# Hybrid encoder block on one core: the value projection and its convolution move behind the attention output's projections, a gate's projection moves beside the attention

## The chip, the cores and the metric

The kernel runs on one core of one Trainium2 chip. The metric is the device time of one execution in microseconds; the time of a kernel is the median of its runs.

## The reference, cut to what matters

One layer over 512 tokens with 1024 features, everything in float32. The normalised input h is multiplied by one wide matrix, whose columns are cut into the parts that the branches use:

```
h  = rmsnorm(x)
aq, ak, av = silu(causal_conv4(h @ W[q, k, v]))     # branch A, 512 columns each
oA = gated_delta_rule(l2norm(aq), l2norm(ak), av, g, beta)   # chunks of 64 tokens
oA = rmsnorm(oA) * silu(h @ W[z])
oB = top-128 attention(h @ W[b_q, b_k, b_v, i_q, i_k, i_w])  # branch B
x  = x + (sigmoid(h @ W[gate_a]) * (oA @ P_A) + sigmoid(h @ W[gate_b]) * (oB @ P_B)) @ W_out
x  = x + mixture_of_experts(rmsnorm(x))             # 16 experts, 2 per token
out = rmsnorm(x)
```

The convolution runs along the tokens over four taps, for each of the 1536 q, k and v features on its own. The delta rule solves one unit-triangular system per head and chunk of 64 tokens.

## The kernel before

**Projections.** A product with 512 columns of W is a "chunk" of four steps. A step takes 256 rows of W (512 KB from memory into a tile `raw`), splits them into a high and a low part (`split`: `whi` on ScalarE, `wlo` on VectorE or, as the string LOWS says, on GpSimd), and issues 24 matmuls, three for each product, into four PSUM banks (`acc`, four buffers). The split of the next step is issued a step ahead. After the last step each bank is evacuated: gate chunks by a Tanh on ScalarE; q, k and v chunks by `conv`; z by a copy, a Tanh and a VectorE product.

**conv.** For each of the four banks ScalarE copies the bank to `xrb` (L448) and a scaled copy to `xh` (L450); VectorE adds three shifted products (L452, 512 columns); after the fourth bank four Silu (L457) write the result. `xh` lies in the four buffers with tag `cv`, as do z's tiles `zt`.

**Order of the chunks.** kv, iq, then beside index scores, selection of keys and attention: bq, qk0, v, qk1, gb0 and gb1. In `behind_projections` each of these 24 steps advances the selection (PICKS), the attention (LOOKS) and the norms (NORMS) by the listed number of pieces. Selection is a chain of VectorE instructions (L595, L596). Then come pb0 and pb1 (attention output by P_B, with `systems`, which builds the triangular systems and sends their diagonal blocks to memory, `lane_n`); ga0 and z; ga1; and the delta rule (`solve`, `chain`).

**sides, lanes, clear_TT, lanes_back.** `sides(g)` has four pieces for each of two groups of heads: four transposes of k and v on TensorE (L920, L921), three VectorE products (L924 to L926), two GpSimd products (L928) and four memsets. `lanes` loads the diagonal blocks (`LN`), inverts them in 31 pairs of VectorE instructions (L952, L953), each of which needs the one before, and writes the result to memory (`lane_x`). `clear_TT` zeroes tiles TT0 and TT1 in the buffers of q and k (kq0, kq1), and TT2 and TT3 in one of h's; `lanes_back` brings the inverses there from `lane_x`, eight DMAs for two tiles. `solve` begins with TT0.

**Who decides the order in a queue.** All instructions are traced first; the framework then writes out each engine's queue: of what its model holds ready, it takes what was traced first. On the chip each engine runs its queue in order.

In the kernel before, `sides` advances by one piece of each group in each step of ga0, and `lanes` by 0, 2, 4, 4 pairs in ga0's steps and 5, 5, 5, 6 in z's.

Of the kernel before, what the change touches and what calls it, by code (L numbers as in the profile page):

```python
# [7 lines left out]
F32 = mybir.dt.float32  # L8
F32R = mybir.dt.float32r
I32 = mybir.dt.int32  # L10
AF = mybir.ActivationFunctionType
OP = mybir.AluOpType
# [6 lines left out]
T = 4  # L19
# [9 lines left out]
SELS = (13, 14)  # L29

LOWS = "DDDDDDDDDDDDPPDPPPPPPPPPPPPPPPPP"
PICKS = (1, 5, 5, 4, 4, 4, 4, 2, 2, 4, 4, 4, 2, 3, 4, 4, 3, 0, 0, 0, 0, 0, 0, 0)
LOOKS = (0, 0, 0, 0, 0, 0, 0, 0, 1, 1, 1, 4, 2, 3, 4, 4, 4, 5, 5, 4, 5, 5, 4, 4)
NORMS = (0, 0, 0, 0, 0, 0, 0, 0, 0, 1, 1, 1, 1, 1, 1, 0, 0, 2, 1, 1, 1, 1, 2, 2)

A_Q, A_K, A_V, A_Z, A_B = 0, 512, 1024, 1536, 2048
B_Q, B_K, B_V, I_Q, I_K, GATE_A, GATE_B = 2064, 2576, 2704, 2832, 3344, 3416, 4440
# [61 lines left out]
def body(tc, x, positions, norm1_g, w_in, w_proj_a, w_proj_b, w_out, norm2_g,  # L99
         w_exp_gate, w_exp_up, w_exp_down, final_norm_g, small, const, out, dbg=None):  # L100
    nc = tc.nc
    dbg = dbg or {}
    PE, ACT, DVE, POOL, SP = nc.tensor, nc.scalar, nc.vector, nc.gpsimd, nc.sync
# [115 lines left out]
    plan, raws, ready, state = [], [], [], {"at": 0, "limit": None}  # L219
    win = w_in[0]  # L220

    def want(key, src, nk, cols, *lo):

        for sub in range(nk // 2):
            plan.append((key, [src[sub * 256:(sub + 1) * 256, c:c + m] for c, m in cols], lo[sub % len(lo)]))

    low = lambda s: [POOL if c == "P" else DVE for c in s]
# [1 line left out]
    want("iq", win, 8, [(I_Q, 512)], *low(LOWS[4:8]))  # L229
    want("bq", win, 8, [(1992, 456)], *low(LOWS[8:12]))  # L230
    want("qk0", win, 8, [(A_Q, 256), (A_K, 256)], *low(LOWS[12:16]))
    want("v", win, 8, [(A_V, 512)], *low(LOWS[16:20]))
    want("qk1", win, 8, [(A_Q + 256, 256), (A_K + 256, 256)], *low(LOWS[20:24]))
    for hf in range(2):
        want(f"gb{hf}", win, 8, [(GATE_B + 512 * hf, 512)], *low(LOWS[24 + 4 * hf:28 + 4 * hf]))
    for hf in range(2):
        want(f"pb{hf}", w_proj_b[0], 4, [(512 * hf, 512)], DVE)
    want("ga0", win, 8, [(GATE_A, 512)], DVE)
    want("z", win, 8, [(A_Z, 456)], DVE)
    want("ga1", win, 8, [(GATE_A + 512, 512)], DVE)  # L240
    for hf in range(2):
# [137 lines left out]
    def tick(bg):  # L379
        for gen, n in bg:  # L380
            for _ in range(n):
                next(gen, None)

    def drain(*gens):
        for g in gens:
            for _ in g:
                pass
# [31 lines left out]
    def feat_chunk(*a, bg=()):  # L419
        for _ in feat_gen(*a):  # L420
            tick(bg)

    HT = lambda k: (hTh[k // 4][:, k % 4, :], hTl[k // 4][:, k % 4, :])
# [3 lines left out]
    cw = SM("conv").rearrange("p (b k) -> p b k", k=4)  # L427
# [10 lines left out]
    vT = [vT2[p // 2][:, p % 2, :] for p in range(4)]  # L438
    kq = [Ft([128, T, 2, 128], F32, f"kq{p}", f"kq{p}") for p in range(4)]

    xrb = Ft([128, 4, 512], F32, "xrb", "tg0")

    waiting = []

    def conv(blk, fb, acc, dst):

        xr = xrb[:, fb]
        ACT.activation(xr, acc, AF.Copy)  # L448
        xh = Ft([128, 512], F32, "xh", "cv", 4)
        out = ins_of(ACT.activation(xh, acc, AF.Copy, scale=cw[:, blk, 3:4]))  # L450
        for j in (1, 2, 3):
            DVE.scalar_tensor_tensor(xh[:, j:], xr[:, :512 - j], cw[:, blk, 3 - j:4 - j], xh[:, j:], op0=OP.mult, op1=OP.add)  # L452
        waiting.append((dst, xh.rearrange("p (t c) -> p t c", t=T) if len(dst.shape) == 3 else xh))
        if fb == 3:
            with after_(out):
                for d, v in waiting:
                    ACT.activation(d, v, AF.Silu)  # L457
            waiting.clear()

    def qk_chunk(g, bg):  # L460
        def ev(fb, acc):
            p = 2 * g + fb % 2
            conv(p if fb < 2 else 4 + p, fb, acc, kq[p][:, :, 1 if fb < 2 else 0, :])
        feat_chunk(f"qk{g}", 8, HT, ev, bg=bg)


# [270 lines left out]
                turn(2 + u // 2)  # L737
            yield from att_value(*res[u])

    gb = [Ft([128, 4, 512], F32, f"gb{hf}", f"tg{hf}") for hf in range(2)]  # L740

    def gate_gen(hf):
        def ev(fb, acc):
            j = 8 + hf * 4 + fb
            ACT.activation(gb[hf][:, fb, :], acc, AF.Tanh, bias=bgh[:, j:j + 1], scale=0.5)
        return feat_gen(f"gb{hf}", 8, HT, ev)
# [5 lines left out]
    def gate_spill(hf):  # L752
        def ev(fb, acc):
            if hf == 0:
                tg = Ft([128, 512], F32, "tga", "cv", 4)
            else:
                if fb % 2 == 0:
                    spare.append(Ft([128, 2, 512], F32, "tga", f"kq{2 + fb // 2}"))
                tg = spare[-1][:, fb % 2]
            ACT.activation(tg, acc, AF.Tanh, bias=bgh[:, hf * 4 + fb:hf * 4 + fb + 1], scale=0.5)  # L760
            SP.dma_start(gad[hf, :, fb, :], tg)
        return feat_gen(f"ga{hf}", 8, HT, ev)
# [4 lines left out]
    def behind_projections():  # L767

        for i, n in enumerate(PICKS):
            tick([(sel, n), (att, LOOKS[i]), (nrm[i // 16], NORMS[i])])  # L770
            yield

    bg = [(behind_projections(), 1)]
    tok_chunk("bq", 8, range(T), HT, ev_w3, bg=bg)
    qk_chunk(0, bg)
    feat_chunk("v", 8, HT, lambda fb, acc: conv(8 + fb, fb, acc, vT[fb]), bg=bg)
    qk_chunk(1, bg)
    drain(nrm[0])
    for _ in gate_gen(0):
        tick(bg)  # L780
    drain(sel)

# [46 lines left out]
    DVE.tensor_tensor(flat(dl), ps[:, 32:64], flat(nG), op=OP.add)  # L829
    ACT.activation(dl, dl, AF.Exp)  # L830

    for _ in gate_gen(1):
        tick(bg)
    drain(att, nrm[1])
    for g in range(2):
# [121 lines left out]
    TT = {}  # L957

    def clear_TT(t):
        if t < 2:  # L960
            TT[t] = Ft([128, 8, 128], F32, f"TT{t}", f"kq{t}")
            POOL.memset(TT[t], 0.0)
        else:
            tt = Ft([128, 2, 8, 128], F32, "TT2", "H10")
            POOL.memset(tt, 0.0)
            TT[2], TT[3] = tt[:, 0], tt[:, 1]

    def lanes_back(tiles):
# [130 lines left out]
    def z_chunk():  # L1099
        def ev(t, acc):  # L1100
            z = Ft([128, 512], F32, f"zt{t}", "cv", 4)
            zt[t] = z
            zg = GP([128, 512], name="zg", tag="E", bufs=2)
            ACT.activation(z[:, 0:456], acc[:, :456], AF.Copy)
            POOL.tensor_copy(z[:, 456:512], ztail[:, t, :])
            ACT.activation(zg, z, AF.Tanh, scale=0.5)
            DVE.scalar_tensor_tensor(z, zg, 1.0, z, op0=OP.add, op1=OP.mult)
        return tok_gen("z", 8, range(T), HT, ev)
# [9 lines left out]
    rk0 = G([128, T, 1024], name="rk0")  # L1118
# [8 lines left out]
    rk1 = [Ft([128, 2, 1024], F32, f"rk1{i}", ("obh", "obl")[i]) for i in range(2)]  # L1127
    place(1, [ke_[1][:, t] for t in range(T)], [rk1[t // 2][:, t % 2] for t in range(T)])
    side, lane = [sides(g) for g in range(2)], lanes()
    for n, _ in zip((0, 2, 4, 4), gate_spill(0)):  # L1130
        tick([(side[0], 1), (side[1], 1), (lane, n)])
    drain(*side)
    for t in range(2):
        clear_TT(t)
    for n, _ in zip((5, 5, 5, 6), z_chunk()):
        tick([(lane, n)])
    drain(lane)

    angz = GP([128, 64], name="angz")
# [2 lines left out]
    for t in range(T):  # L1142
        zv = zt[t].rearrange("p (h d) -> p h d", h=8)
        POOL.tensor_tensor(zv, zv, angz[:, None, :].to_broadcast([128, 8, 64]), op=OP.mult)
    lanes_back((0, 1))
    drain(gate_spill(1))
    feed(state["at"] + 2)
    clear_TT(2)
    lanes_back((2, 3))
# [101 lines left out]
    for fb in range(4):  # L1251
        acc = acc_tile()
# [24 lines left out]
    nm, ex, sums, wn = e1([T, 2], "nm"), e1([T, 24], "exl"), e1([T, 3], "sums"), e1([T, 16], "wn")  # L1277
# [84 lines left out]
    for sub in range(4):  # L1362
        feed(NIN + sub + 2)
        hi, lo, n = ready[NIN + sub]
# [336 lines left out]
    for e in range(16):  # L1701
        acc = acc_tile()
# [110 lines left out]
```

## Time and profile before

| | |
|---|---|
| median of 3 runs | 702.06 us (698.96 to 703.22) |
| the profiled execution | 701.66 us, span of the core 699.8 us |
| TensorE busy in the span | 655.5 us |
| VectorE busy | 526.5 us |
| ScalarE busy | 411.6 us |
| GpSimd busy | 205.0 us |
| granted TensorE clock, mean | 0.980 |

The span is the time from the first to the last instruction of the profiled execution; the other 1.86 us lie around it. The granted clock is the share of TensorE's full speed. Matmuls of 512 columns are recorded with some 0.39 us each but start every 0.23 us, so a busy TensorE need not be a TensorE at its best.

### The profile page before, as it was taken

The numbers are of one execution on the slowest core, as the hardware profiler recorded it, in microseconds if no ns is written. First come the engines' busy times: TensorE is split into PE (matmuls) and PEld (weight loads), VectorE is DVE, ScalarE is ACT, GpSimd is POOL, SyncE is SP. The second block draws the span as 40 slices with busy tenths as digits, with TensorE's granted clock in tenths as the row PEclk, the third lists the DMA queues.
The fourth block names the chain that finished last, engine by engine and source line by source line (L and its number), as shares of the span: only waits on it lengthen the run. The fifth ranks groups of instructions, "written<-read, shape, count | busy, mean of one in ns | idle before, by whom it ended". The sixth has DMA issues, their size and how long they took to land.

```text
span 699.8 us, 10563 instructions
## 1 busy us (share of the span) xinstructions
PE 655.5 (94%) x3460; PEld 538.0 (77%) x3460; DVE 526.5 (75%) x1166; ACT 411.6 (59%) x734; POOL 205.0 (29%) x259
## 2 busy tenths in 40 slices
PE   3999999799899999999999999989999999999992
PEld 2888777567676777778889988878887888888871
DVE  4567799999956466569934666774689999999875
ACT  5345456398968965433333432344258998999863
POOL 2000327516322303231071111660151432333102
PEclk9999999999899999999999999999999999999996
DMA  8333311113021112234355002979779999998963
GB/s 271 118 96 102 91 60 61 60 32 92 29 90 31 61 60 69 76 92 133 92 149 192 2 2 94 380 231 303 256 252 338 333 297 302 300 279 269 282 230 123
DMA packets 84026, 110.77 MB, mean 158 GB/s; under 512 B 17435, under 2 KB 57883, under 8 KB 83840
## 3 DMA queue, kind: packets, MB, share of 16 engines
q1 hardware_dynamic: 79360, 101.70, 44.4%
q0 software_dynamic: 4320, 7.77, 4.5%
q8 instruction: 28, 0.46, 0.3%
q10 hardware_dynamic: 288, 0.59, 0.3%
q14 instruction: 30, 0.25, 0.1%
HBM read 101.22 MB, written 16.78 MB: 169 GB/s over the span
## 4 chain that ended last, share of the span: by engine, by line
PE 70%; DVE 16%; ACT 4%; issue 4%; POOL 3%; DMA 2%; POOLq 0%; ACTq 0%; DVEq 0%
PE acc L129 53%; PE pm L129 7%; DVE xh L452 3%; PE pm L1546 2%; DVE sn L596 2%; DVE ltmp L952 2%; PE po L129 2%; DVE m L595 1%; DVE wlo L154 1%; DVE X L953 1%; POOL wlo L154 1%; POOL mTl L1227 1%; DMA xe<-h2d,ids 1%; PE pg L129 1%; PE ssq L129 1%
## 5 line engine op out<-in xcount | busy, mean ns | idle before, releaser
L153 ACT ACTIVATE whi<-raw 128x1024 fp32r<-128x1024 f32 (+1 forms) x123 | 126.7, 1048 | 99.1 <-PE acc L129 81.2
L154 DVE TENSOR_TENSOR wlo<-raw,whi 128x1024 fp32r<-128x1024 f32 (+1 forms) x100 | 124.1, 1264 | 45.1 <-ACT whi L153 35.3
L154 POOL TENSOR_TENSOR wlo<-raw,whi 128x1024 fp32r<-128x1024 f32 x23 | 57.2, 2489 | 124.6 <-ACT whi L153 116.6
L129 PE MATMUL acc<-whi,xhl 128*128 128x512 f32 x256 | 91.3, 410 | 0.3 <-DVE xhl L1553 0.3
L129 PE MATMUL acc<-hTh,wlo 128*128 128x512 f32 x224 | 89.3, 400 | 1.7 <-POOL wlo L154 1.1
L129 PE MATMUL acc<-hTh,whi 128*128 128x512 f32 x224 | 89.9, 402 | 0.8 <-ACT zb L649 0.8
L129 PE MATMUL acc<-hTl,whi 128*128 128x512 f32 x224 | 89.0, 397 | 0.0
L129 PEld LDWEIGHTS acc<-whi,xhl 128*128 128x128 f32 x256 | 48.1, 188 | 10.2 <-DVE xhl L1553 0.8
L129 PEld LDWEIGHTS acc<-hTh,wlo 128*128 128x128 f32 x224 | 42.6, 190 | 11.6 <-POOL wlo L154 1.7
L129 PEld LDWEIGHTS acc<-hTh,whi 128*128 128x128 f32 x224 | 42.8, 191 | 10.1 <-ACT zb L649 1.0
L129 PE MATMUL acc<-wlo,xhl 128*128 128x512 f32 x128 | 50.4, 394 | 0.0
L129 PEld LDWEIGHTS acc<-hTl,whi 128*128 128x128 f32 x224 | 42.8, 191 | 9.0 <-issue 0.9
L129 PE MATMUL acc<-whi,hTh 128*128 128x456 f32 (+1 forms) x120 | 45.5, 386 | 0.0
L129 PE MATMUL acc<-whi,hTl 128*128 128x456 f32 (+1 forms) x120 | 45.1, 376 | 0.0
L129 PE MATMUL acc<-wlo,hTh 128*128 128x456 f32 (+1 forms) x120 | 44.8, 374 | 0.1
L1591 POOL DMA_INDIRECT accd<-yb,ids x14 | 23.9, 1705 | 58.7 <-ACT ah L153 58.7
L1390 POOL DMA_INDIRECT xe<-h2d,ids x15 | 22.5, 1498 | 42.6 <-PE pm L1546 35.9
L452 DVE SCALAR_TENSOR_TENSOR xh<-xrb,sm,xh 128x511 f32<-128x511 f32 (+2 forms) x36 | 29.8, 879 | 0.0
L129 PE MATMUL acc<-whi,mTh 128*128 128x512 f32 (+1 forms) x72 | 27.9, 388 | 1.8 <-DVE ma L1221 1.8
L595 DVE MAX8 m<-sn 128x8 f32<-128x256 f32 (+2 forms) x48 | 26.6, 557 | 1.1 <-POOL sn L588 0.3
L129 PE MATMUL acc<-whi,mTl 128*128 128x512 f32 (+1 forms) x72 | 27.2, 378 | 0.0
L129 PEld LDWEIGHTS acc<-wlo,xhl 128*128 128x128 f32 x128 | 24.2, 189 | 3.7
(469 smaller groups left out, 1615.6 us busy)
## 6 DMA issues: line engine op xcount, KB each, us to landing
raw<-in_w_in_dram SPq DMA_DIRECT2D x24, 512.0 KB
raw<-in_w_exp_gate_dram SPq DMA_DIRECT2D x42, 256.0 KB
raw<-in_w_exp_up_dram SPq DMA_DIRECT2D x42, 256.0 KB
raw<-in_w_exp_down_dram SPq DMA_DIRECT2D x21, 512.0 KB
raw<-in_w_in_dram SPq DMA_DIRECT2D x16, 256.0 KB
raw<-in_w_out_dram SPq DMA_DIRECT2D x8, 512.0 KB
raw<-in_w_in_dram SPq DMA_DIRECT2D x8, 456.0 KB
x<-in_x_dram SPq DMA_DIRECT2D x4, 512.0 KB
```

What stands on the lines that cost most here:

```text
L129: return ins_of(PE.matmul(o, l, r, start=start, stop=stop, skip_group_check=True))
L153: h = ins_of(ACT.activation(hi, src, AF.Copy))
L154: return h, ins_of((lo_eng or DVE).tensor_tensor(lo, src, f32(hi), op=OP.subtract))
L452: DVE.scalar_tensor_tensor(xh[:, j:], xr[:, :512 - j], cw[:, blk, 3 - j:4 - j], xh[:, j:], op0=OP.mult, op1=OP.add)
L595: DVE.max(m8, sn[t])
L596: DVE.match_replace(out=sn[t], in_to_replace=m8, in_values=sn[t], imm_value=-2 * BIG)
L952: DVE.tensor_tensor(tv, skew(flat[0], 0, n, d, 1), skew(flat[1], d, n, d, 32), op=OP.mult)
L953: state["lanes"] = ins_of(DVE.tensor_reduce(skew(flat[0], d, n, 1, 1), tv, axis=AX.X, op=OP.add))
L1227: state["mTl"] = POOL.tensor_tensor(mTl[j][:, i], ma[:, cs], f32(hi[:, cs]), op=OP.subtract)
L1390: return ins_of(POOL.indirect_dma_start(out=xe, out_offset=None, in_=h2d[0:128 * tiles], in_offset=bass.IndirectOffsetOnAxis(ap=idc, axis= ...
L1546: PE.transpose(ps[:, d * 128:(d + 1) * 128], xe[:, k * 128:(k + 1) * 128], C("ident"))
L1591: return ins_of(POOL.indirect_dma_start(out=accd, out_offset=bass.IndirectOffsetOnAxis(ap=idc, axis=0), in_=y, in_offset=None, bounds_chec ...
```

## The change

The v chunk leaves its place beside the attention, and gb0 takes it; qk1 follows, gb1 takes gb0's place and ga0 takes gb1's. After pb1 stand v, z and ga1. The convolution's VectorE part becomes a generator, `conv_sums`: for q and k it is run out at once after the fourth bank, for v its first block follows the v chunk and one block each of the others follows z's first three steps, ahead of the lanes. `lanes` advances by 0, 5, 6, 6 pairs in v's steps and 4, 4, 3, 3 in z's. `sides` moves behind z, two pieces of each group in ga1's first two steps; then TT0 and TT1 are cleared and lanes_back((0, 1)) is issued, still within ga1. `xrb` lies in gb1's buffer for q and k, and for v in the part of `rk0` that holds tokens 256 to 511 of group 0. LOWS is unchanged, so the steps beside the attention keep their splits on GpSimd, whichever columns they hold. PICKS and LOOKS are changed from the thirteenth and the eleventh step on.

```diff
-PICKS = (1, 5, 5, 4, 4, 4, 4, 2, 2, 4, 4, 4, 2, 3, 4, 4, 3, 0, 0, 0, 0, 0, 0, 0)
-LOOKS = (0, 0, 0, 0, 0, 0, 0, 0, 1, 1, 1, 4, 2, 3, 4, 4, 4, 5, 5, 4, 5, 5, 4, 4)
+PICKS = (1, 5, 5, 4, 4, 4, 4, 2, 2, 4, 4, 4, 4, 4, 4, 4, 0, 0, 0, 0, 0, 0, 0, 0)
+LOOKS = (0, 0, 0, 0, 0, 0, 0, 0, 1, 1, 2, 4, 4, 4, 4, 2, 3, 5, 5, 5, 5, 5, 5, 5)
...
-    want("v", win, 8, [(A_V, 512)], *low(LOWS[16:20]))
+    want("gb0", win, 8, [(GATE_B, 512)], *low(LOWS[16:20]))
...
+    want("gb1", win, 8, [(GATE_B + 512, 512)], *low(LOWS[24:28]))
+    want("ga0", win, 8, [(GATE_A, 512)], *low(LOWS[28:32]))
...
-    want("ga0", win, 8, [(GATE_A, 512)], DVE)
+    want("v", win, 8, [(A_V, 512)], DVE)
...
-        for j in (1, 2, 3):
-            DVE.scalar_tensor_tensor(xh[:, j:], xr[:, :512 - j], cw[:, blk, 3 - j:4 - j], xh[:, j:], op0=OP.mult, op1=OP.add)
...
+    def conv_sums(blocks, out):
+        for n, (blk, xr, xh, dst) in enumerate(blocks):
+            for j in (1, 2, 3):
+                DVE.scalar_tensor_tensor(xh[:, j:], xr[:, :512 - j], cw[:, blk, 3 - j:4 - j], xh[:, j:], op0=OP.mult, op1=OP.add)
+            if n < len(blocks) - 1:
+                yield
+        with after_(out):
+            for blk, xr, xh, dst in blocks:
+                ACT.activation(dst, ..., AF.Silu)
+        yield
...
-    feat_chunk("v", 8, HT, lambda fb, acc: conv(8 + fb, fb, acc, vT[fb]), bg=bg)
+    for _ in gate_gen(0):
+        tick(bg)
     qk_chunk(1, bg)
     drain(nrm[0])
-    for _ in gate_gen(0):
+    gb.append(Ft([128, 4, 512], F32, "gb1", "tg1"))
+    for _ in gate_gen(1):
         tick(bg)
     drain(sel)
...
-    for _ in gate_gen(1):
+    for _ in gate_spill(0):
         tick(bg)
...
-    for n, _ in zip((0, 2, 4, 4), gate_spill(0)):
-        tick([(side[0], 1), (side[1], 1), (lane, n)])
-    drain(*side)
-    for t in range(2):
-        clear_TT(t)
-    for n, _ in zip((5, 5, 5, 6), z_chunk()):
+    state["xrb"] = rk0[:, 2:4].rearrange("p t (b c) -> p (t b) c", c=512)
+    for n, _ in zip((0, 5, 6, 6), feat_gen("v", 8, HT, lambda fb, acc: conv(8 + fb, fb, acc, vT[fb]))):
         tick([(lane, n)])
+    tick([(sums[-1], 1)])
+    for n, _ in zip((4, 4, 3, 3), z_chunk()):
+        tick([(sums[-1], 1), (lane, n)])
     drain(lane)
...
-    lanes_back((0, 1))
-    drain(gate_spill(1))
+    for n, _ in zip((2, 2, 0, 0), gate_spill(1)):
+        if n:
+            tick([(side[0], n), (side[1], n)])
+        else:
+            drain(*side)
+            if not TT:
+                for t in range(2):
+                    clear_TT(t)
+                lanes_back((0, 1))
```

## Rows read from the trace of the kernel before

**Rows 1.** The page: busy us (share of the span) and instructions of each engine.
```profile
PE 655.5 (94%) x3460; PEld 538.0 (77%) x3460; DVE 526.5 (75%) x1166; ACT 411.6 (59%) x734; POOL 205.0 (29%) x259
```
**Rows 2.** Windows beside the attention: length, busy us of PE, PEld, DVE, ACT, POOL, clock.
```profile
120.00:132.00 12.00, 6.48 (x22) 4.38 (x21) 11.51 (x27) 5.90 (x11) 9.05 (x8) 0.88 0.28 85
...
141.00:157.00 16.00, 14.29 (x65) 10.17 (x64) 15.90 (x42) 15.71 (x34) 2.70 (x2) 1.00 0.09 30
...
178.00:188.00 10.00, 7.96 (x37) 5.97 (x35) 9.91 (x19) 9.97 (x25) 0.00 (x0) 0.96 0.00 0
188.00:200.00 12.00, 11.57 (x44) 9.77 (x44) 9.07 (x33) 6.02 (x10) 5.62 (x3) 0.75 0.29 88
200.00:212.00 12.00, 11.00 (x53) 8.39 (x52) 6.18 (x17) 10.67 (x22) 3.91 (x7) 1.00 0.15 44
212.00:261.00 49.00, 48.40 (x231) 35.36 (x230) 26.32 (x73) 38.49 (x75) 10.14 (x13) 1.00 0.17 54
```
**Rows 3.** TensorE's waits from 82 to 266 us: total, times, longest.
```profile
PE pm L129 <- DVE sn L586: 4.2, 2, 3.9
PE po L129 <- ACT ph L153: 1.9, 1, 1.9
```
**Rows 4.** The chain that ended last, from 140 to 212 us: start, us, what.
```profile
154.30 2.38 POOL wlo L154
...
180.60 5.26 DVE xh L452 x8
```
**Rows 5.** Windows of ga0, z and ga1, columns as in rows 2.
```profile
302.00:325.40 23.40, 23.40 (x118) 19.55 (x117) 18.44 (x46) 6.56 (x11) 2.49 (x11) 1.00 0.31 85
325.40:348.60 23.20, 22.54 (x110) 19.61 (x109) 22.20 (x45) 7.47 (x11) 3.33 (x6) 1.00 0.35 117
348.60:370.40 21.80, 21.80 (x103) 18.12 (x103) 8.22 (x17) 8.80 (x12) 14.73 (x20) 1.00 0.50 142
```
**Rows 6.** VectorE's timeline, the convolution's sums: start, length, instructions.
```profile
107.50 11.72 DVE L452 SCALAR_TENSOR_TENSOR xh<-xrb,sm,xh 128x510 f32<-128x510 f32 x10
...
147.69 4.71 DVE L452 SCALAR_TENSOR_TENSOR xh<-xrb,sm,xh 128x510 f32<-128x510 f32 x7
```
**Rows 7.** Groups of instructions by line: count, busy us, mean ns, idle before.
```profile
L154 DVE TENSOR_TENSOR wlo<-raw,whi 128x1024 fp32r<-128x1024 f32 (+1 forms) x100 | 124.1, 1264 | 45.1 <-ACT whi L153 35.3 <-PE pm L129 9.1 <-issue 0.3
...
L450 ACT ACTIVATE xh<-acc,sm 128x512 f32<-128x512 f32 x12 | 8.2, 684 | 0.0
...
L448 ACT ACTIVATE xrb<-acc 128x512 f32<-128x512 f32 x12 | 7.1, 592 | 3.5 <-PE acc L129 3.5
```
**Rows 8.** ScalarE's timeline at the end of the v chunk.
```profile
148.56 1.28 ACT L457 ACT_TABLE_LOAD   x1
149.85 1.15 ACT L457 ACTIVATE vT<-xh 128x512 f32<-128x512 f32 x2
```
**Rows 9.** VectorE's timeline: the first and the last lane instruction, two of sides.
```profile
310.79 0.22 DVE L952 TENSOR_TENSOR ltmp<-X,LN 128x31 f32<-128x31 f32 x1 [0.77 <-DMA LN<-lane_n]
...
313.48 0.41 DVE L925 TENSOR_TENSOR rk<-pm,kds 128x256 f32<-128x256 f32 x1
313.81 0.41 DVE L926 TENSOR_TENSOR rk<-pm,scv 128x256 f32<-128x256 f32 x1
...
353.58 0.18 DVE L953 TENSOR_REDUCE X<-ltmp 128x1 f32<-128x31 f32 x1
```
**Rows 10.** GpSimd's timeline: clearing TT0 and TT1, z's products after the lanes.
```profile
325.56 1.86 POOL L962 MEMSET TT<- 128x1024 f32 x2 [18.15 <-PE pm L920]
...
354.04 5.90 POOL L1144 TENSOR_TENSOR zt<-zt,angz 128x512 f32<-128x512 f32 x4 [23.89 <-DVE angz L1141]
```
**Rows 11.** SyncE's queue: the inverses' way out and back.
```profile
353.83 0.34 SPq L955 DMA_DIRECT2D lane_x<-X  x1
...
358.60 3.79 SPq L971 DMA_DIRECT2D TT<-lane_x  x8
```
**Rows 12.** GpSimd's timeline beside the convolution of q and k.
```profile
112.92 1.18 POOL L504 TENSOR_TENSOR ropeB<-bq,sin 128x256 f32<-128x256 f32 x1
```

More of the change, by code (lines that the diff above doesn't have):

```diff
@@ L231, in body @@
     want("qk0", win, 8, [(A_Q, 256), (A_K, 256)], *low(LOWS[12:16]))
-    want("v", win, 8, [(A_V, 512)], *low(LOWS[16:20]))
+    want("gb0", win, 8, [(GATE_B, 512)], *low(LOWS[16:20]))
     want("qk1", win, 8, [(A_Q + 256, 256), (A_K + 256, 256)], *low(LOWS[20:24]))
-    for hf in range(2):
-        want(f"gb{hf}", win, 8, [(GATE_B + 512 * hf, 512)], *low(LOWS[24 + 4 * hf:28 + 4 * hf]))
+    want("gb1", win, 8, [(GATE_B + 512, 512)], *low(LOWS[24:28]))
+    want("ga0", win, 8, [(GATE_A, 512)], *low(LOWS[28:32]))
     for hf in range(2):
         want(f"pb{hf}", w_proj_b[0], 4, [(512 * hf, 512)], DVE)
-    want("ga0", win, 8, [(GATE_A, 512)], DVE)
+    want("v", win, 8, [(A_V, 512)], DVE)
     want("z", win, 8, [(A_Z, 456)], DVE)
@@ L439, in body @@
     kq = [Ft([128, T, 2, 128], F32, f"kq{p}", f"kq{p}") for p in range(4)]
-    xrb = Ft([128, 4, 512], F32, "xrb", "tg0")
-    waiting = []
+    state["xrb"] = Ft([128, 4, 512], F32, "xrb", "tg1")
+    waiting, sums = [], []
     def conv(blk, fb, acc, dst):
-        xr = xrb[:, fb]
+        xr = state["xrb"][:, fb]
         ACT.activation(xr, acc, AF.Copy)
@@ L450, in conv @@
         out = ins_of(ACT.activation(xh, acc, AF.Copy, scale=cw[:, blk, 3:4]))
-        for j in (1, 2, 3):
-            DVE.scalar_tensor_tensor(xh[:, j:], xr[:, :512 - j], cw[:, blk, 3 - j:4 - j], xh[:, j:], op0=OP.mult, op1=OP.add)
-        waiting.append((dst, xh.rearrange("p (t c) -> p t c", t=T) if len(dst.shape) == 3 else xh))
+        waiting.append((blk, xr, xh, dst))
         if fb == 3:
-            with after_(out):
-                for d, v in waiting:
-                    ACT.activation(d, v, AF.Silu)
+            sums.append(conv_sums(list(waiting), out))
             waiting.clear()
+    def conv_sums(blocks, out):
[6 more added lines that the diff above has]
+            for blk, xr, xh, dst in blocks:
+                ACT.activation(dst, xh.rearrange("p (t c) -> p t c", t=T) if len(dst.shape) == 3 else xh, AF.Silu)
+        yield
     def qk_chunk(g, bg):
@@ L463, in ev @@
             conv(p if fb < 2 else 4 + p, fb, acc, kq[p][:, :, 1 if fb < 2 else 0, :])
+            if fb == 3:
+                drain(sums[-1])
         feat_chunk(f"qk{g}", 8, HT, ev, bg=bg)
@@ L738, in attention @@
             yield from att_value(*res[u])
-    gb = [Ft([128, 4, 512], F32, f"gb{hf}", f"tg{hf}") for hf in range(2)]
+    gb = [Ft([128, 4, 512], F32, "gb0", "tg0")]
     def gate_gen(hf):
```

## The prediction

> **What bounds the kernel now.** The page's first part comes first: TensorE is busy 655.5 of 699.8 us, VectorE 526.5 [rows 1]. TensorE's own work is the same before and after (a v chunk and a gate chunk have the same matmuls, and the transposes of `sides` only move), so the change can win or lose only what TensorE waits, and what its clock is low. The windows say where that is. Beside the attention, from 120 us on, TensorE's busy time falls short of the window in all five windows shown before 212 us, and after that by 0.6 us in 49 [rows 2]. In the short ones VectorE is full (11.51 of 12, 15.90 of 16, 9.91 of 10), and from 141 to 157 us and from 178 to 188 us ScalarE is full too (15.71 of 16, 9.97 of 10). The list of waits confirms it: the largest is for a sum of index scores on VectorE (4.2 us), the next for ScalarE's high half of an attention weight (1.9 us) [rows 3]. The chain that ended last runs through VectorE and ScalarE there, and at 180.60 us through eight sums of qk1's convolution, 5.26 us [rows 4]. In ga0, z and ga1 TensorE is nearly gapless (67.74 us busy of 68.40), but VectorE fills z's window (22.20 of 23.20) and has only 8.22 of 21.80 us to do in ga1's [rows 5]. So v's convolution lies where VectorE and ScalarE limit, and is moved to where VectorE is full for 20 us more and then free.
>
> **Part 1: what leaves the attention.** Twelve sums of v: 4.71 us for seven, 0.67 each, make 8.1 us of VectorE [rows 6]. On ScalarE four copies and four scaled copies, 4 x (0.592 + 0.684) = 5.1 us [rows 7], four Silu at 0.58, 2.3 us, and two table loads (to Silu and back) at 1.28, 2.6 us [rows 8]: 10.0 us. The Tanh of the gate chunk that comes instead is four instructions of a bank, by the scaled copy's 0.684 us 2.7 us. Net relief: 8.1 us of VectorE, 7.3 us of ScalarE. GpSimd's splits stay.
>
> The Trainium skill, page "ScalarE: Activation LUTs", section "What ACT_TABLE_LOAD costs", puts 1.38 us of drain behind each load of 1.28 us. The trace doesn't show it: the load at 148.56 us lasts 1.28 us, and the Silu starts at 149.85 [rows 8]. By the page the relief on ScalarE would be 10.1 us instead of 7.3.
>
> **What TensorE gets of that.** Up to 141 us nothing changes: the same instructions, the same PICKS and LOOKS up to the tenth step, and qk0's convolution as before. The longest wait, 3.9 us [rows 3], and the clock of 0.88 from 120 to 132 us [rows 2] stay: 0. From 141 to 157 us TensorE stands 16 - 14.29 = 1.7 us; there the v chunk's evacuation keeps ScalarE from the next split, whose low part runs on GpSimd at 154.30 us on the chain [rows 4]. I take all of it: -1.7 (bounds 0 and -1.7). From 178 to 212 us it stands 2.0 + 0.4 + 1.0 = 3.5 us, and 12 us at a granted clock of 0.75, that is partly at 1.2 instead of 2.4 GHz, behind the idle stretch before, cost 12 x 0.25 = 3.0 us more [rows 2]: 6.5 in all. Its cause, qk1's sums and Silu in one burst on the chain [rows 4], stays; but VectorE comes to it with 8.1 us less behind it, and LOOKS puts 2 and 3 pieces of attention there instead of 4 and 4. I take half, -3.2 (bounds 0 and -6.5). Behind 212 us nothing is left to win. Sum: -4.9 (0 to -8.2).
>
> **Part 2: what comes to the lanes.** The 31 pairs of lanes run from 310.79 to 353.76 us, 43.0 us [rows 9]. VectorE is full in them, and 18 of the 24 products of sides lie between, 0.33 us from start to start [rows 9], 5.9 us. They go; v's twelve sums come, 8.1 us, and one more split, 1.26 us [rows 7]: 43.0 - 5.9 + 8.1 + 1.3 = 46.5 us. The first lane ran 8.8 us after its chunk's start (302.00 [rows 5] to 310.79), when the blocks' way through memory was done; that way begins in pb1 as before. So the lanes end 55.3 us after the start of v. For the sums this trace has a second price: seven took 0.67 us each, but ten beside qk0, while GpSimd turned queries, 11.72 us, 1.17 each [rows 6]. By it lanes end at 61.3. I take the first: GpSimd is busy only 2.49 and 3.33 us in these two windows [rows 5].
>
> TensorE needs 68.4 us for the three chunks with the transposes [rows 5], so 13.1 us are left behind the lanes' end (7.1 by the second price; 16.6 before, to 370.40). In this time VectorE does all 24 products of sides, 24 x 0.33 = 7.9 us, and two splits, 2.5 us: 10.4, it fits. TT0 and TT1 lie in the buffers of q and k of group 0, and can be cleared after the sixth of the eight pieces: 5.9 + 2.5 = 8.4 us. z's products on GpSimd (5.90 us) are over by then, the clearing takes 1.86 us [rows 10], TT0's four DMAs half of 3.79 us [rows 11]: 12.2 us. What one then needs to land isn't shown; it lies between 0 and 4.8 us, the time from the write of `lane_x` to the first issue behind it [rows 11]. `solve` needs TT0 at 13.1: from 0.9 early to 3.9 late. I take 1.5 late, nearer to the early end, since 4.8 us holds a whole write of 512 KB. SyncE's queue holds weight loads behind those DMAs, five steps ahead; at this wait they cost nothing.
>
> Two smaller terms. z's fourth bank is copied into a buffer that v's last Silu frees, and VectorE does the last of v's sums before the last six pairs of lanes. At 43.0/31 = 1.4 us a pair that is 55.3 - 8.3 = 47.0, with Silu and copy 48.2 us. v and z take TensorE 21.8 + 23.2 = 45.0 us [rows 5], and ga1's first step reaches its fourth bank 4.1 us later: no wait (by the second price 5.1). The transposes of sides stand in TensorE's queue among ga1's first steps, and their three PSUM banks are emptied by a VectorE that is on lanes until 10.3 us into ga1. If the order written in advance takes lanes to be shorter than they are, TensorE stands; z's window shows 0.66 us of such standing [rows 5]. Bounds 0 and 4; I take 1.0, by that row.
>
> ga0's chunk, gb1's buffer (free 20 us before it is written) and the four spills cost nothing: their cover is a whole chunk of some 22 us. Sum of part 2: +2.5 (0 to 3.9 + 5.1 + 4 = +13).
>
> **Sum.** 701.66 us for the profiled execution (span 699.8, 1.86 around it) - 4.9 + 2.5 = 699.3 us. That execution lies 0.4 us under the median of 702.06. Less than 1%, 7 us, can hardly be told from no change here.
>
> **Rivals.** *All waits go.* With VectorE 8.1 us ahead, the selection ends before qk1's burst, TensorE never stands behind it and keeps its clock, and the inverses come back in time: 701.66 - 8.2 = 693.5 us. For it: VectorE and ScalarE are both full in just these windows [rows 2]. Against it: qk1's burst itself isn't smaller. Chance 0.20.
>
> *The relief isn't used.* qk1's sums hold attention as before, 141 to 157 us win little, and the lanes' stage pays: -0.5 + 4, 705 us. For it: the largest wait has qk0's convolution before it, not v's. Chance 0.20.
>
> *The lanes become the bound (slower).* VectorE runs v's sums at 1.17 us, the lanes end at 61.3, TT0 lands 61.3 + 12.2 to 17.0 = 73.5 to 78.3 us after v's start against 68.4: 5 to 10 us late, say 7.5. After such an idle stretch the clock costs 3.0 us, as after 188 us [rows 2]. With 1.7 won: 701.66 - 1.7 + 7.5 + 3.0 = 710.5 us. It decides where the write of `lane_x` is issued less than 12 us before ga1's last matmul. For it: GpSimd's products of 1.18 us beside the slow sums [rows 12] show that the two engines hold each other up. Against it: little runs on GpSimd in the new place. Chance 0.13. The Trainium skill, page "SBUF — State Buffer", section "Who interferes with whom", has a rule of this kind: a VectorE instruction with two SBUF inputs and a GpSimd instruction that reads SBUF exclude each other. By it the four GpSimd products of sides that must wait for v's sums, and z's, could fall on lanes; the slow sums and slow products in the rows agree with it.
>
> **How the numbers follow.** Forecast 699.3 us with 0.47, its own range 696 to 703. 692 to 708 us takes in the rivals but the slower one and the far ends of the others, and leaves out some 0.17. Faster by over 1% (under 695.0): most of the first rival and a little of the forecast, 0.23. Slower by over 1% (over 709.1): most of the last, 0.11. Between: 0.66.
>
> **What would show it.** Right: from 141 to 157 us TensorE's idle time falls under 0.5 us; no Silu table load between qk0's and qk1's; the lanes take 45 to 48 us, with twelve sums at 0.67 us among them; the products of sides follow in ga1; solve's first matmul waits 0 to 3 us. Wrong: the stop at some 185 us and the low clock behind it remain whole, or grow with the denser LOOKS; lanes past 50 us; or TensorE standing for VectorE in ga1.

## The result, and the profile after

The changed kernel takes 709.28 us, median of four runs (708.54 to 710.16), against 702.40 for the kernel before beside it (698.96 to 703.22): a ratio of 1.0121, 95% interval 1.0093 to 1.0150. It is slower by 1.2%; forecast were 699.3 us. The profiled execution takes 709.65 us, its span is 707.8 us against 699.8.

The page's busy times, for [rows 1]: TensorE's work is the same, so the 8 us are waits and clock.

```profile
PE 657.2 (93%) x3460; PEld 541.6 (77%) x3460; DVE 527.5 (75%) x1166; ACT 411.3 (58%) x734; POOL 207.5 (29%) x259
```

Three marks of TensorE divide them: the first matmul out of the attention's output (`obh`, pb0) came at 260.8 us before and comes at 263.3 after; the first one out of TT (`solve`) at 369.1 and 378.6. So the attention's stage ends 2.4 us later (forecast: 4.9 sooner), pb, v, z and ga1 together take 7.1 us more (forecast 2.5), and what follows takes 1.5 us less.

*The attention.* Windows of the changed kernel, in the order of [rows 2]; the last is 2.3 us longer.

```profile
120.00:132.00 12.00, 6.44 (x22) 4.28 (x21) 11.66 (x27) 6.57 (x12) 9.21 (x8) 0.86 0.27 82
141.00:157.00 16.00, 13.01 (x51) 10.03 (x51) 12.63 (x39) 11.80 (x33) 5.08 (x6) 0.79 0.17 51
178.00:188.00 10.00, 9.69 (x44) 7.67 (x43) 9.94 (x26) 9.05 (x19) 2.57 (x1) 1.00 0.17 51
188.00:200.00 12.00, 8.50 (x33) 6.51 (x31) 10.26 (x22) 8.58 (x13) 5.90 (x2) 0.86 0.20 56
200.00:212.00 12.00, 12.00 (x58) 8.79 (x57) 6.39 (x20) 11.41 (x25) 3.45 (x6) 1.00 0.17 58
212.00:263.30 51.30, 50.36 (x242) 38.16 (x241) 26.04 (x72) 38.05 (x75) 12.65 (x15) 1.00 0.20 68
```

From 120 to 132 us nothing moved, as forecast. From 141 to 157 us ScalarE now has some 4 us to spare, as the relief should leave it. VectorE's 3.4 idle us are no such slack: 2.74 of them are the wait for GpSimd shown below, and where that wait is gone (e2 and e3 below) VectorE is busy 15.6 of 16 us (15.90 before). TensorE stands 2.99 us instead of 1.71, at a granted clock of 0.79 instead of 1.00 (a mean between its two levels, 1.2 and 2.4 GHz). From 178 to 212 us it stands 0.31 + 3.50 + 0 = 3.8 us (3.5 before); the idle time has moved from the first of the three windows to the second. TensorE's waits from 82 to 264 us, for [rows 3]:

```profile
PE pm L129 <- DVE sn L596: 4.3, 2, 3.9
PE pm L129 <- DVE mx L680: 3.2, 2, 3.0
PE acc L129 <- POOL wlo L154: 1.8, 1, 1.8
PE acc L129 <- ACT whi L153: 1.7, 1, 1.7
```

The second to fourth are new in this size. TensorE's timeline has them at 149.73, 195.54 and 192.35 us, and a fifth wait in ga1:

```profile
149.73 1.11 PE L129 MATMUL pm<-bkk,bqs 128*128 128x128 f32 x4 [2.99 <-DVE mx L680]
...
192.35 0.50 PE L129 MATMUL acc<-hTh,whi 128*128 128x512 f32 x1 [1.73 <-ACT whi L153]
195.54 0.50 PE L129 MATMUL acc<-hTh,wlo 128*128 128x512 f32 x1 [1.77 <-POOL wlo L154]
...
352.92 0.27 PE L933 MATMUL pm<-cst,vT 128*128 128x128 f32 x1
...
358.00 0.45 PE L932 MATMUL pm<-cst,kq 128*128 128x128 f32 x1 [3.88 <-DVE rk L938]
```

What stands behind the first of them is in GpSimd's timeline: six products that turn the query tile of attention unit 2 run from 139.35 us, and the clearing of 64x64 index scores comes behind them, at 143.63 us. In the kernel before it stood at 140.32 us.

```profile
139.35 0.74 POOL L513 TENSOR_TENSOR ropeA<-bq,cos 128x256 f32<-128x256 f32 x1
...
142.96 0.74 POOL L516 TENSOR_TENSOR bq<-ropeA,ropeB 128x256 f32<-128x256 f32 x1
143.63 0.14 POOL L598 MEMSET sn<- 64x64 f32 x1
...
182.64 2.57 POOL L154 TENSOR_TENSOR wlo<-raw,whi 128x1024 fp32r<-128x1024 f32 x1 [6.63 <-ACT whi L153]
```

VectorE's timeline shows who waits for it, then qk1's sums, and last the lanes:

```profile
143.81 0.69 DVE L605 MAX8 m<-sn 128x8 f32<-128x512 f32 x1 [2.74 <-POOL sn L598]
...
182.97 2.28 DVE L821 TENSOR_SCALAR beta<-beta 128x32 f32<-128x32 f32 x1
...
186.57 6.70 DVE L460 SCALAR_TENSOR_TENSOR xh<-xrb,sm,xh 128x510 f32<-128x510 f32 x10
193.19 0.55 DVE L680 CUSTOM_DVE_ANT_0 l<-pm,sn 128x384 f32<-128x384 f32 x1
...
313.19 0.21 DVE L964 TENSOR_TENSOR ltmp<-X,LN 128x31 f32<-128x31 f32 x1 [2.32 <-DMA LN<-lane_n]
...
356.47 0.41 DVE L936 TENSOR_TENSOR rk<-pm,eG 128x256 f32<-128x256 f32 x1
...
357.25 0.17 DVE L965 TENSOR_REDUCE X<-ltmp 128x1 f32<-128x31 f32 x1
```

VectorE's next MAX8 waits 2.74 us for the clearing, and the attention's row maxima (L680) queue behind it: TensorE's 2.99 us. At 186.57 us ten of qk1's sums run without a break, and a row maximum of the attention comes only behind them. On ScalarE the Silu of these sums, with a table load, stand ahead of the weight splits (`whi`) for which TensorE waits at 192.35 us:

```profile
188.72 1.28 ACT L465 ACT_TABLE_LOAD   x1 [1.46 <-DVE xh L460]
190.01 1.33 ACT L465 ACTIVATE kq<-xh 128x512 f32<-128x512 f32 x2
191.25 1.99 ACT L153 ACTIVATE whi<-raw 128x1024 fp32r<-128x1024 f32 x2
```

The lanes run from 313.19 to 357.4 us, 44.2 us (forecast 46.5), with v's twelve sums at 0.77 us among them, and end 53.0 us after v's start (forecast 55.3).

*v, z, ga1.* Windows for [rows 5], and two inside ga1:

```profile
304.40:326.40 22.00, 22.00 (x99) 18.28 (x99) 14.90 (x33) 9.25 (x16) 1.96 (x9) 1.00 0.31 93
326.40:347.00 20.60, 19.86 (x94) 17.06 (x93) 20.36 (x35) 9.97 (x14) 4.79 (x8) 1.00 0.25 77
347.00:378.60 31.60, 27.72 (x126) 22.64 (x125) 20.32 (x51) 7.82 (x11) 14.77 (x18) 0.89 0.33 96
...
353.00:359.00 6.00, 2.12 (x11) 1.63 (x10) 5.72 (x21) 0.00 (x0) 1.30 (x2) 0.84 0.35 135
359.00:366.00 7.00, 7.00 (x23) 5.49 (x23) 3.53 (x7) 0.22 (x1) 5.63 (x6) 0.65 0.35 110
```

v and z run as forecast. The loss behind the attention is in ga1: TensorE stands 3.88 us before the fourth transposed piece of `sides`, at 358.00 us, because three pieces fill the three PSUM banks by 352.92 us and VectorE frees none before its first product at 356.47 us. The granted clock of 0.65 behind that costs 7 x 0.35 = 2.5 us more.

### The profile page after: what moved, and what is told of

It reads as the page before. It is cut to its first block, busy times and chain, and to the rows that moved or that the text cites. A ratio compares the mean times of both kernels' runs of the same rounds, so it can differ in the third digit from the quotient of the medians.

```text
span 707.8 us, 10554 instructions
## 1 busy us (share of the span) xinstructions
PE 657.2 (93%) x3460; PEld 541.6 (77%) x3460; DVE 527.5 (75%) x1166; ACT 411.3 (58%) x734; POOL 207.5 (29%) x259
## 4 chain that ended last, share of the span: by engine, by line
PE 69%; DVE 17%; ACT 4%; POOL 3%; issue 3%; DMA 2%; ACTq 0%; POOLq 0%; DVEq 0%; SPq 0%
PE acc L129 52%; PE pm L129 7%; DVE xh L460 3%; DVE sn L606 2%; DVE m L605 2%; PE pm L1565 2%; DVE wlo L154 2%; DVE ltmp L964 2%; PE po L129 1%; POOL wlo L154 1%; POOL mTl L1246 1%; DMA xe<-h2d,ids 1%; DVE X L965 1%; PE pm L708 1%; PE pg L129 1%
## 5 line engine op out<-in xcount | busy, mean ns | idle before, releaser
L129 PE MATMUL acc<-hTl,whi 128*128 128x512 f32 x224 | 90.5, 404 | 0.0
L129 PE MATMUL acc<-wlo,mTh 128*128 128x512 f32 (+1 forms) x72 | 26.4, 367 | 0.0
```

The source lines that it names most:

```text
L129: return ins_of(PE.matmul(o, l, r, start=start, stop=stop, skip_group_check=True))
```

## The experiments

"Stage end" is the first matmul out of `obh`, "solve" the first out of TT, both in us of the profiled execution; the ratio is to the kernel before on the same chip. The runs were made on several chips, on which the kernel before took 701.57 to 703.70 us, so rows are compared by their ratios.

| kernel | median us | ratio, 95% interval | stage end | solve |
|---|---|---|---|---|
| before | 702.40 | 1 | 260.8 | 369.1 |
| changed | 709.28 | 1.0121 [1.0093, 1.0150] | 263.3 | 378.6 |
| e1_sides_later | 703.50 | 1.0027 [0.9998, 1.0055] | 263.2 | 372.6 |
| e2_look_one | 709.07 | 1.0113 [1.0062, 1.0165] | 262.8 | 376.9 |
| e3_mask_dve | 709.41 | 1.0109 [1.0057, 1.0162] | 260.9 | 375.5 |
| c1_before_look | 703.27 | 1.0021 [0.9999, 1.0043] | 265.5 | 373.7 |
| e5_sides_mask | 702.99 | 1.0004 [0.9977, 1.0032] | 262.6 | 372.1 |
| e6_sides_spread | 699.09 | 0.9945 [0.9927, 0.9963] | 258.5 | 368.0 |
| e7_sides_oldsteps | 706.12 | 1.0020 [0.9992, 1.0048] | 262.7 | 372.1 |
| e8_all | 696.77 | 0.9915 [0.9887, 0.9942] | 256.4 | 365.9 |
| e9_silu_late | 712.49 | 1.0162 [1.0129, 1.0194] | 272.2 | 381.5 |
| c2_before_both | 705.00 | 1.0061 [1.0035, 1.0087] | 265.0 | 373.2 |
| e10_both_spread | 707.41 | 1.0105 [1.0051, 1.0158] | 264.6 | 374.1 |
| c3_before_grouped | 702.95 | 0.9995 [0.9976, 1.0013] | 262.0 | 370.3 |

A stage end in one execution is good to some 2 us: e3 and e5 have the same queues up to it, and end it at 260.9 and 262.6, with a granted clock of 0.86 and 0.67 from 120 to 132 us.

**The transposes in ga1.** In the changed kernel, `sides` is moved down ga1, group 0 into its second step and group 1 into its third, with the clearing and fetching of TT0 and TT1 right behind group 0:

```
-    for n, _ in zip((2, 2, 0, 0), gate_spill(1)):
-        if n:
-            tick([(side[0], n), (side[1], n)])
-        else:
-            drain(*side)
-            if not TT:
-                for t in range(2):
-                    clear_TT(t)
-                lanes_back((0, 1))
+    for n, _ in zip((0, 1, 2, 3), gate_spill(1)):
+        if n == 1:
+            drain(side[0])
+            for t in range(2):
+                clear_TT(t)
+            lanes_back((0, 1))
+        elif n == 2:
+            drain(side[1])
```

> The changed kernel with one edit in ga1's stage: the transposes of sides stand behind ga1's second and third step (group 0 first, with the clearing and the fetching of TT0 and TT1 right behind it) instead of its first and second. Theory A (TensorE's queue): the 3.88 us for which TensorE stands at 358 us is only a matter of place, since three of the four transposed pieces fill the three PSUM banks, VectorE empties none before it is through with the lanes at 357 us, and ga1's third step stands behind the fourth piece; the granted clock of 0.65 from 359 to 366 us follows from that standing and cost 7 x 0.35 = 2.5 us. Both go: 709.3 - 6.4 = 702.9 us, no wait over 1 us in ga1, first matmul of solve 72 to 74 us after the start of v's first one. Rival B (the way through memory): the end of the lanes sets the end of the stage in any case; the write of lane_x, the clearing of TT0 and its four transfers (issued at 368.15 us now) end last, and the wait moves to solve's first matmul: 707 to 709 us, with a wait of 4 us or more on TT.

Theory A. The time is 703.50 us, 5.8 less (the ratio falls from 1.0121 to 1.0027), and solve comes 68.4 us after v's start (304.2). The window of ga1, answering to the third one above:

```profile
346.60:372.60 26.00, 25.44 (x127) 20.67 (x127) 20.99 (x52) 7.84 (x11) 13.71 (x19) 1.00 0.37 98
```

TensorE stands 0.6 us in it instead of 3.9, at full clock. The way of the inverses through memory isn't late even then.

**The clearing behind the turned queries.** Three kernels: the changed one with LOOKS 10 to 12 at `1, 4, 5` (was `2, 4, 4`); the changed one with

```
-        POOL.memset(s[0:64, N - 64:N], -BIG)
+        DVE.memset(s[0:64, N - 64:N], -BIG)
```

and the kernel before with LOOKS 10 to 12 at `2, 4, 1` (was `1, 4, 2`).

> The changed kernel with LOOKS 10 to 12 at 1, 4, 5 instead of 2, 4, 4: one piece of attention a step later, the sum unchanged. GpSimd's queue then has the clearing of the masked part of tile 3's scores ahead of the turning of the third query tile, as the kernel before had it. Theory A (GpSimd's queue): VectorE's 2.74 us and TensorE's 2.99 us at 149.7 us behind that clearing go, and with them the granted clock of 0.79 from 141 to 157 us (16 x 0.21 = 3.4 us): 709.3 - 3 to -6, about 705 us, clock over 0.95 in that window. Rival B (VectorE is full there with or without it): TensorE waits for the same sums a little later, 708.5 to 710 us, and the window's clock stays under 0.85.

> The changed kernel with its LOOKS unchanged, and the clearing of the masked part of the index scores done by VectorE instead of GpSimd (three instructions of 64x64). Theory A (GpSimd's queue): it does the same as the earlier place in GpSimd's queue, about 705 us, with the denser LOOKS left in. Rival B (the denser LOOKS put too much of the attention on VectorE at this place): 708.5 to 710 us, TensorE still stands 2 us or more behind the row maximum at 150 us.

> The kernel before with LOOKS 10 to 12 at 2, 4, 1 instead of 1, 4, 2 and nothing else: v stays where it was. GpSimd's queue then has the turning of the third query tile ahead of the clearing of tile 3's scores, as the changed kernel has it. Theory A: this one step makes the wait without the move of v: 702.4 + 2 to 5 us, about 705.5, with TensorE standing 2 to 3 us behind the row maximum near 150 us and a lower clock behind it. Rival B (the wait comes from gb0 in v's place): 702 to 703 us, no such wait.

At the place itself theory A holds in all three. The window from 141 to 157 us of e2, then that of e3:

```profile
141.00:157.00 16.00, 14.42 (x66) 10.28 (x65) 15.62 (x42) 12.78 (x34) 7.98 (x8) 1.00 0.20 61
```

```profile
141.00:157.00 16.00, 15.20 (x70) 10.73 (x69) 15.63 (x45) 13.51 (x36) 5.77 (x6) 1.00 0.19 57
```

and TensorE's wait in c1, where v has not moved:

```profile
150.65 0.44 PE L129 MATMUL pm<-bkk,bqs 128*128 128x128 f32 x2 [3.21 <-DVE mx L670]
```

So one piece of attention a step earlier makes the wait by itself, and the place in GpSimd's queue is its cause. For the time theory A fails: e2 and e3 can't be told from the changed kernel, nor c1 from the kernel before, though with four runs each of e2 and e3 a gain of 2 us isn't excluded. What e3 wins by 157 us it gives back in part from 188 to 200 us, where TensorE is busy 7.66 us of 12 at a clock of 0.72, against 8.50 at 0.86. In its one profile the stage still ends 2.4 us sooner; behind `solve` that execution takes 331.5 us against 329.2.

**The two together, and the old steps.** e5 is e1 with e3's edit; e7 is e1 with PICKS and LOOKS of the kernel before.

> Both edits together: sides behind ga1's second and third step, and the scores' clearing on VectorE. The two earlier runs ended the attention's stage at 263.2 us (sides alone) and 260.9 us (clearing alone, but the same total time). Theory A (the two parts add up): the first matmul of solve comes 2.4 us sooner than with sides alone, at 370 us, and the time is 703.5 - 2.4 = 701 us. Rival B (what the attention wins is given back behind it, as the total of the clearing alone said): 703 to 704 us.

> Sides behind ga1's second and third step, with PICKS and LOOKS of the kernel before. This is the move of v with the selection and the attention at their old steps. The prediction's reasoning (VectorE and ScalarE relieved of v's convolution) expects its gain here, if the new steps were what undid it: attention ends at 256 to 259 us, 697 to 700 us. Rival B (the relief is not used, since TensorE waits for the attention's own chain): attention ends at 261 to 264 us, 702 to 704 us.

Rival B in both: neither can be told from e1 by its ratio (e7's median of 706.12 us lies above both ranges; its nine runs lie from 701.12 to 707.08). In e7 the largest of TensorE's waits from 120 to 266 us is for the high half of attention weights, 4.9 us in three. In e5 the place is qk1's burst; VectorE's timeline, TensorE's, and the window:

```profile
183.90 9.59 DVE L460 SCALAR_TENSOR_TENSOR xh<-xrb,sm,xh 128x509 f32<-128x509 f32 x8
193.41 0.55 DVE L680 CUSTOM_DVE_ANT_0 l<-pm,sn 128x384 f32<-128x384 f32 x1
...
197.67 0.17 DVE L821 TENSOR_SCALAR beta<-beta 128x32 f32<-128x32 f32 x1
```

```profile
194.02 1.01 PE L129 MATMUL pm<-bkk,bqs 128*128 128x384 f32 x2 [4.32 <-DVE mx L680]
```

```profile
188.00:200.00 12.00, 7.42 (x26) 6.02 (x27) 9.51 (x24) 8.63 (x16) 3.69 (x7) 0.72 0.30 88
```

**qk1's burst.** In e6 (on e1) and e8 (on e5) the twelve sums no longer stand in one piece (in e8's trace the longest run of them is six, 4.05 us):

```
-            if fb == 3:
+            if fb == 3 and g == 0:
                 drain(sums[-1])
...
-    gb.append(Ft([128, 4, 512], F32, "gb1", "tg1"))
-    for _ in gate_gen(1):
+    for i, _ in enumerate(gate_gen(1)):
+        tick([(sums[-1], (1, 2, 1, 0)[i])])
+        if i == 2:
+            gb.append(Ft([128, 4, 512], F32, "gb1", "tg1"))
         tick(bg)
```

with NORMS 17 at 0 instead of 2.

> Sides behind ga1's second and third step, and qk1's twelve convolution sums no longer in one burst at the end of its chunk but spread over gb1's first three steps (1, 2, 1 blocks), its Silu behind the third, the norms of the second group up to two steps later. Theory A (the burst): VectorE's burst of sums and the table load that ScalarE does behind it, ahead of gb1's next weight split, make the two waits of 1.8 us from 188 to 200 us and the clock of 0.86 there; spread, they go, and the attention ends at 258 to 260 us instead of 263.2: 703.5 - 3 to -5 = 699.5 us. Rival B (VectorE has as much to do in any order): the waits move to gb1's other steps, attention ends at 262 to 264 us, 703 to 704 us.

> All three edits: sides later, clearing of the scores on VectorE, qk1's sums spread. If the waits at 150 us and at 190 us are separate and each costs what its windows show, the attention ends at 257 to 259 us and the time is 697 to 699 us. If the attention is held by VectorE's sum of work, it ends at 261 us or later, and the time is 701 to 703 us.

Theory A. The stage of e6 ends 4.7 us sooner than that of e1, and its ratio falls from 1.0027 to 0.9945; with the clearing out of GpSimd's queue as well, e8 takes 696.77 us, faster than both kernels. The two waits are separate: all five runs of e8 lie below all nine of e6, by 2.3 us in the median. With the burst left in place the clearing's gain doesn't show (e5 against e1, e3 against the changed kernel); whether it is smaller there or only lost in the spread of the runs isn't shown. Windows of e8:

```profile
157.00:178.00 21.00, 20.55 (x103) 16.32 (x104) 20.55 (x58) 14.97 (x37) 9.11 (x9) 1.00 0.18 51
178.00:188.00 10.00, 8.75 (x40) 7.02 (x39) 9.84 (x22) 6.48 (x14) 3.82 (x2) 1.00 0.22 58
188.00:200.00 12.00, 9.97 (x50) 7.81 (x49) 11.86 (x23) 11.91 (x23) 6.78 (x7) 1.00 0.18 49
200.00:212.00 12.00, 12.00 (x59) 9.52 (x58) 6.87 (x21) 11.51 (x24) 3.35 (x2) 1.00 0.33 91
```

TensorE still stands 3.3 us from 178 to 200 us, but in pieces of at most 1.25 us, and its granted clock is 1.00 throughout.

e9 asks which half of the burst it was. It is e8 with the sums back in one piece and only the Silu held back, behind a later weight split:

```
+            if fb == 3:
+                tick([(sums[-1], 4)])
...
+        if i == 2:
+            state["hold"] = state["hi"]
+            tick([(sums[-1], 1)])
```

> Sides later and the scores' clearing on VectorE (703.0 us, attention's stage to 262.6 us), and of the spreading of qk1's convolution only the half on ScalarE: the twelve sums stay in one burst behind qk1's chunk, the Silu and its table load are issued behind a later weight split of gb1 (the attention's Exp in between costs two more table loads). Theory A (VectorE's burst is what stops TensorE from 188 to 200 us): no gain, attention to 260 to 264 us, 701 to 704 us. Theory B (the Silu and its table load, which wait for the sums with the next weight split behind them on ScalarE): the gain of spreading comes back, attention to 256 to 258 us, 697 to 698 us.

```profile
188.00:200.00 12.00, 7.36 (x26) 5.99 (x27) 9.95 (x25) 1.69 (x5) 3.01 (x2) 0.72 0.30 88
```

TensorE's busy time is e5's to 0.06 us and the clock is the same, with ScalarE busy 1.69 us instead of 8.63: in e5's order the sums stop TensorE there, not the Silu or its table load. In the changed kernel itself TensorE waits at this place for the splits behind the Silu (192.35 and 195.54 us), and no run holds back the Silu alone there. e9's steps of the norms are e8's, so these aren't it either. The stage ends later than expected under either theory, at 272.2 us: ScalarE, which has the held Silu and their table loads to do, comes to gb1's Tanh only at 226.58 us, and TensorE waits 3.96 us for a bank. As a version it is worth nothing.

e10 is e8 with qk0's sums spread in the same way over gb0, behind the index scores.

> The version with all three edits (696.8 us), and qk0's twelve sums spread too, behind the index scores of gb0's steps instead of ahead of them (the norms of the first group two steps later). Theory A (a burst of sums ahead of the scores is what makes the longest wait, 3.9 us at some 124 us, and the clock of 0.88 behind it): the wait falls under 1.5 us, the attention ends at 251 to 254 us instead of 256.4, 692 to 694 us. Rival B (the selection's steps move up into the place of the sums and hold the scores as long): the wait stays at 3 us or more, 696 to 698 us.

```profile
120.00:132.00 12.00, 9.47 (x43) 6.87 (x42) 11.70 (x24) 7.26 (x10) 6.34 (x6) 1.00 0.27 82
132.00:141.00 9.00, 6.52 (x31) 5.10 (x30) 9.00 (x16) 5.29 (x9) 8.38 (x7) 1.00 0.21 60
```

Neither theory: the time, 707.41 us, lies far above both. TensorE stands 2.5 us in the first window at full clock (5.1 us at 0.91 in e8), but 2.5 us more in the second (0 in e8), with VectorE busy 9.00 of 9. The stage ends 8 us later than e8's, and that loss lies further on: TensorE stands 2.96 us from 141 to 157 us (0.81 in e8) and 3.49 us from 212 to 260 us (0.18). That VectorE has no slack to spread into here would explain it, but no run tests this.

**What the move of v is worth.** c2 and c3 are the kernel before with e3's edit and the spreading, over gb0's steps: `(1, 2, 1, 0)` in c2, `(0, 4, 0, 0)` in c3.

> The kernel before, v at its old place, with the two edits in the attention that brought the changed kernel from 703.5 to 696.8 us: the scores' clearing on VectorE, and qk1's sums spread over the next chunk's first three steps, with the norms' steps that go with it. Theory A (moving v relieves the attention once qk1's burst is out of the way, as the prediction's 4.9 us said): the edits win less here, since VectorE still has v's twelve sums: attention to 259 to 262 us (260.8 before), 700 to 704 us. Rival B (the two edits do it alone, and the move of v is worth nothing): 696 to 698 us, attention to 255 to 257 us.

c2 doesn't decide it: its Silu fell into three groups with a table load each, and TensorE stood behind them. (The next expectation counts three such loads and two of Exp from 204 to 217 us; in the trace two and one lie there, the first Silu's is at 186.56 us.)

```profile
217.33 0.79 PE L129 MATMUL po<-ph,vhl 128*128 128x512 f32 x1 [5.13 <-ACT ph L153]
```

> As the earlier control (the kernel before, v at its old place, scores cleared by VectorE, qk1's sums behind gb0's steps), but all twelve sums behind gb0's second step, so that ScalarE has the four Silu in one group with one table load; the earlier one had three loads of Silu and two of Exp in between from 204 to 217 us, and TensorE stood 5.13 us for a high half behind them. Theory A (moving v relieves the attention by about the 4.9 us of the prediction, once qk1's burst is out of the way): without the move the attention ends at 259 to 262 us, against 256.4 with it, and the time is 700 to 703 us. Rival B (the order of qk1's sums is all, the move of v gives the attention nothing): it ends at 255 to 257 us, 695 to 698 us.

By its numbers theory A: c3's stage ends at 262.0 us, 5.6 later than e8's, and its time can't be told from the kernel before. Two of its windows, where e8's above are nearly full, and VectorE's timeline in the second:

```profile
157.00:178.00 21.00, 18.34 (x86) 13.82 (x87) 20.25 (x46) 16.05 (x40) 11.69 (x10) 1.00 0.27 75
...
200.00:212.00 12.00, 9.88 (x49) 7.57 (x47) 11.69 (x23) 10.31 (x18) 5.01 (x3) 1.00 0.15 44
```

```profile
199.46 6.86 DVE L460 SCALAR_TENSOR_TENSOR xh<-xrb,sm,xh 128x510 f32<-128x510 f32 x7
206.36 0.56 DVE L680 CUSTOM_DVE_ANT_0 l<-pm,sn 128x384 f32<-128x384 f32 x1
```

TensorE stands 2.7 and 2.1 us in them, e8's 0.45 and 0, with VectorE at 11.69 of 12 us in the second against 6.87. But the second window holds seven of qk1's sums in one piece with a row maximum behind them, for which TensorE waits 2.10 us: c3 has a burst again, which e8 has not, and the two also differ in PICKS and LOOKS. So the 0.8% between them (0.9915 against 0.9995) is the worth of the whole version, not of the move of v, which no run here measures by itself. What is shown is less: the same two edits, in the two orders tried, win nothing with v at its old place.

## Why the prediction was wrong

*What bounds the kernel* was read rightly: the loss, too, is all waits and clock of TensorE, and the relief of VectorE and ScalarE by v's work is real. The gain of 4.9 us forecast from it didn't appear: by one profile each the attention's stage ends 2.4 us later, and e1, in which ga1's loss is gone, can't be told from the kernel before. (The 5.6 us between the stages of c3 and e8 are near the forecast, but not by the move alone.) Two steps failed there, and a third in ga1, which made nearly all of the measured loss.

*"From 141 to 157 us ... I take all of it: -1.7 (bounds 0 and -1.7)."* This step failed. The prediction noted that LOOKS is the same only up to the tenth step, and didn't follow the eleventh, 1 to 2, into GpSimd's queue: it brings six products ahead of a clearing of 0.14 us that VectorE's selection waits for. It measured 1.3 us more of standing and up to 16 x 0.21 = 3.4 us of clock at this place; in the whole time, taking the wait away wins 2.3 us from e6 to e8 and nothing measurable in e2, e3 and e5. The bound at 0 was the mistake behind it: nothing excluded a loss. That v's evacuation made the wait is not borne out either: in e2, with the old queue order and no v, TensorE's busy time is 14.42 of 16 us, and was 14.29.

*"From 178 to 212 us ... I take half, -3.2."* This failed too. By the windows the cost there went from 6.5 us to 3.8 + 12 x 0.14 = 5.5, so 1.0 was won. The cause was named rightly, qk1's sums in one burst, but the half was taken on the ground that VectorE comes to it with less behind it. The burst has the attention's row maxima behind it, whatever lies ahead; e6 and e8 win only by taking it apart, and e9 shows for e5's order that it is the sums.

*"Bounds 0 and 4; I take 1.0"* for the transposes of sides: the mechanism was the right one and the size wrong. They measured 3.88 us of standing, near the upper bound of 4, and 2.5 us of clock behind it, which the term left out; e1 gives 5.8 us for both. The sum was in the text: lanes end 55.3 us after v's start, 10.3 us into ga1, and the pieces stood in ga1's first two steps. The term was taken from a row of z's window instead.

*Right* were: no change up to 141 us; the lanes' length and end, with v's sums at 0.77 us each in the record (forecast 0.67 from start to start; not the 1.17 of the second price); z's fourth bank; and that ga0's chunk and gb1's buffer cost nothing. TT0, forecast 1.5 us late, wasn't late, even in e1 with ga1 5.6 us shorter. e1's 68.4 us from v to solve are the prediction's 68.4 for these three chunks.

The slower rival gave 710.5 us, near the result, by a mechanism that didn't occur: the lanes didn't become the bound.

Left open: what the move of v is worth by itself; and what holds e7 back (with the old steps and no v its stage ends at 262.7 us), beyond the list of its waits. e7 too still has qk1's sums in one piece, and its longest wait, 2.94 us at 191.17 us, is for a high half that ScalarE makes behind their Silu. The 1.5 us that the stages behind `solve` take less than in the profile of before are within the spread: in the fourteen profiles these stages take 328.0 to 332.0 us.

## What to carry to other kernels

A relief of a full engine pays only at the wait that ends last. Follow each instruction that a changed pacing moves into every in-order queue, GpSimd's too, and look for a short instruction there that another engine's chain waits for. Long bursts of work without urgency (a convolution's sums) ahead of short urgent work (row maxima) are worth taking apart where the engine has slack behind them (e6, e8); the one try where it was full (e10) lost. Transposes in TensorE's queue whose banks an engine frees only later belong behind that point, and a stop of TensorE is priced with the low clock behind it.

## What was unexpected in the hardware

An instruction on VectorE can take over ten times its time beside a split on GpSimd. `beta`, 128x32, takes 0.17 us in e5, at 197.67 us with GpSimd idle, and 2.28 us in the changed kernel, from 182.97 us; it ends at 185.25, as the split that began at 182.64 ends (185.21). qk1's sums took 0.67 us each in the changed kernel's ten at 186.57 us, with GpSimd idle until 192.37, and 9.59 / 8 = 1.20 us in e5, with two splits beside them. That makes the burst longer where the attention waits for its end. The Trainium skill, page "SBUF — State Buffer", section "Who interferes with whom", says that the two engines share a port pair, that a VectorE instruction with two SBUF inputs contends with a GpSimd instruction that reads SBUF, that a `tensor_scalar` in a two-port mode contends with GpSimd too, and that the one that issues second is fully blocked for the whole of the other. `beta`'s row agrees to 0.04 us. For the sums no run here changes GpSimd's splits alone, so this stays an agreement of rows.
